# Second half of the mixing projection row tile by row tile, with part of its weights loaded during the merge and later element-wise work moved to VectorE

## The chip, the core and the metric

The kernel runs on one core of a Trainium2 chip. The metric is the time of one execution in microseconds (us), measured on the device. TensorE is called PE, VectorE DVE, ScalarE ACT, GpSimd POOL and SyncE SP, as in the profile. SP, POOL and ACT also issue DMAs from queues that each work in their own order.

## The reference

One layer of a streaming encoder on x of 1024 x 1024 in float32, with weights of the layer and a conditioning vector that gives shifts, scales and gates.

```python
h = _layer_norm(x) * (1.0 + sc1) + sh1
q_a, k_a, v_a, f_a, q_c, k_c, v_c, gate_a, gate_c = jnp.split(h @ w_in[l], split_points, axis=-1)
o_a = _forgetting_attention(...)
o_c = _chunk_band_attention(...)
merged = (jax.nn.sigmoid(gate_a) * (o_a @ w_br_fox[l]) + jax.nn.sigmoid(gate_c) * (o_c @ w_br_chunk[l]))
mix = merged @ w_out[l]
x = _layer_norm(alpha * x + (1.0 + g1) * mix, ln1_g[l], ln1_b[l])
h = _layer_norm(x) * (1.0 + sc2) + sh2
u = _causal_depthwise_conv(h @ w_up[l], conv_w[l], conv_b[l])
a, val = jnp.split(u, 2, axis=-1)
y = (jax.nn.silu(a) * val) @ w_down[l]
x = _layer_norm(alpha * x + (1.0 + g2) * y, ln2_g[l], ln2_b[l])
```

The lines that matter here are the merge, the mix, the first LayerNorm, and the start of the FFN (`h @ w_up`).

## The kernel before, in words

Every float32 operand of a product is parted into a high part (a cast) and a low part (the operand less its high part), and every product is made of three matmuls, high by high, high by low and low by high, on 128 x 512 tiles. So a step needs a cast (mostly on ACT) and a subtraction (on DVE or POOL) before PE can start. Weights that the kernel has already parted in DRAM are read back as two 512 KB tiles, `wh` and `wl`, by `parted_w`; of each three such pairs, one lies in tiles called `ws`.

The 1024 rows are handled in two halves of 512. `merge(half)` makes eight products (c = 0 to 7) of the two branch outputs with the branch weights `brd[c]`, each from one weight pair and one gate tile `sgl`; DVE multiplies by the gate (`sgl`), adds, and parts the result into `mh` and `ml`. `mix(half)` multiplies the eight merged tiles by the eight steps of `w_out` (`wod[k]`, k = 0 to 7) into eight PSUM tiles: four row tiles of 128 rows, two halves of 512 columns each, called `psm`. Then, for each row tile, DVE makes the residual sum into `xr`, whose rows of x were loaded by SP.

In the first half all steps run over all four row tiles. In the second half (mix 1), steps 0 to 3 run over all row tiles, and steps 4 to 7 tile by tile, with weights in a pool `wide` that is opened only once the attention outputs' pool is closed, at the end of merge 1. Beside mix 1, `turned_0` transposes the first half's normalised rows on PE into the FFN operands `ha`, `hb`. `norms(half)` applies the first LayerNorm with its gain and bias (`l1g`, `l1b`), stores the rows to `xd`, and normalises them once more into x tiles. For the first half this lies beside merge 1; for the second half it lies after mix 1, beside the first four `head` calls. A `head(c)` is one of eight early products of the FFN, 24 matmuls into `psu`, which use only the first half's operands; `ready(c)` loads and parts its weights. `EARLY = 4` heads run before the second half's operands exist.

After that `turned_1` transposes the second half's rows and forms, for each of four column tiles j, five parted operands: the tile itself (h_22) and four sums or differences (h_t1 to h_t4), with `put` doing the difference (`ht`), the cast and the low part (`hc`). The remaining four heads are interleaved with it. Then the pools `th` and `mxb`, which hold those sums, are closed, and the memory becomes weight tiles `wx` of the FFN loop, whose products (L851) fill the rest of the program. All instructions are placed on their engines in one order by a scheduler at build time; an engine never overtakes itself, nor does a DMA queue.

Of the kernel before, what the change touches and what calls it, by code (L numbers as in the profile page):

```python
# [19 lines left out]
P = 128  # L20
# [15 lines left out]
EARLY = 4  # L36
# [8 lines left out]
def body(ctx, tc, a, out):  # L45
# [814 lines left out]
    def ready(c):  # L860
        if c < HEAD:
            w11, w12 = raw(c, 0, wp, "ws")
            raws.clear()
            lo = ve if c >= EARLY else po
            readied.append((operand(head_slot, mxb, w11, lo=lo), operand(head_slot, mxb, w12, lo=lo)))

    def head(c):
        w11, w12 = readied.pop(0)
        p1 = None
        for i in range(2):  # L870
            ps = product((w11, w12)[i], (h_11, h_21)[i])
            if c < EARLY:
                t = mxb.tile([P, H], F32, name=nm("mc"), tag="h32", bufs=4)
            else:
                t = yp.tile([P, H], F32, name=nm("mc"), tag="mc", bufs=3)
            if i == 0:
                se.copy(out=t, in_=ps)
                p1 = t
            else:
                ve.tensor_tensor(out=t, in0=ps, in1=p1, op=ALU.add)  # L880
            se.dma_start(out=md[c, i], in_=t)
        ready(c + 2)

    if True:
# [11 lines left out]
        def merge(half, os_, beside):  # L896
# [15 lines left out]
            for c in range(KD):  # L912
# [9 lines left out]
                for _ in range(3):  # L922
                    next(beside, None)
            return ms

        def mix(half, ms, beside, wide=None, ended=None):
# [5 lines left out]
            def add(t, k, w):  # L932
                mh, ml = ms[k]
                ts = slice(t * P, (t + 1) * P)
                for n in range(2):
                    pe.matmul(ps[t][n], mh[:, ts], w[0][:, n, :], start=k == 0, stop=False)
                    pe.matmul(ps[t][n], mh[:, ts], w[1][:, n, :], start=False, stop=False)
                    pe.matmul(ps[t][n], ml[:, ts], w[0][:, n, :], start=False, stop=k == KD - 1)

            late = []  # L940
            for k in range(KD):
                last = wide and k >= KD - 4
                w = parted_w(wod[k], wide if last else None)
                if last:
                    late.append((k, w))
                    continue
                for t in range(4):
                    add(t, k, w)
                next(beside, None)
            xs = []  # L950
            for t in range(4):
# [3 lines left out]
                xs.append(xx)  # L955
            for t in range(4):
# [11 lines left out]
        def norms(half, xs, xn):  # L968
            for t, xx in enumerate(xs):
                if half:  # L970
                    normalise(xx, xx, True)
                    ve.tensor_tensor(out=xx, in0=xx, in1=l1g, op=ALU.mult)
                    yield
                    po.tensor_tensor(out=xx, in0=xx, in1=l1b, op=ALU.add)
                else:
                    mv, r = norm_scale(xx)
                    ve.scalar_tensor_tensor(out=xx, in0=xx, scalar=mv[:, 0:1], in1=l1g, op0=ALU.subtract, op1=ALU.mult)
                    ve.scalar_tensor_tensor(out=xx, in0=xx, scalar=r, in1=l1b, op0=ALU.mult, op1=ALU.add)
                    yield
# [34 lines left out]
        def turned_1(tiles):  # L1014
            for j in range(4):
# [5 lines left out]
                t1 = put(h_t1[j], x, h11, ALU.subtract, (ve, se, po), th, 6)  # L1021
                t2 = put(h_t2[j], y, t1, ALU.subtract, (ve, se, po), th, 6)
                put(h_t3[j], y, x, ALU.subtract, (po, se, ve), th, 6)
# [10 lines left out]
        x0, x1 = [], []  # L1034
        beside = norms(0, xs0, x0)
        m1 = merge(1, o1, beside)
# [3 lines left out]
        wide_cm, wide = opened(name="wide", bufs=4, side="right")  # L1040
# [4 lines left out]
        ready(0)  # L1045
        ready(1)
# [5 lines left out]

    mx_cm.__exit__(None, None, None)
    wide_cm.__exit__(None, None, None)
# [377 lines left out]
```

## Time and profile before

| | value |
|---|---|
| median of three runs | 1600.44 us |
| the runs | 1605.11, 1599.81, 1600.44 us |
| profiled execution | 1605.72 us, span 1603.9 us |
| PE busy in the span | 1521.6 us (95%), 7663 instructions |
| DVE busy | 1080.8 us (67%) |
| ACT busy | 712.5 us (44%) |
| POOL busy | 687.1 us (43%) |
| mean granted PE clock | 0.979 of full speed |
| moved by DMA | 317.81 MB, mean 198 GB/s |

The span is the stretch of the profile from the first to the last instruction; the profiled execution's time is 1.8 us longer. Times of stretches below are us from the start of the span. Busy shares are means over stages with different limits, so they say little on a single stage.

### The profile page before, as it was taken

The page shows a single profiled execution, that of the slowest core. Times are in us where ns is not written, and L with a number is a line of the kernel's source. Part 1 is how long each engine was busy: PE and PEld are TensorE (multiplying, and loading weights), DVE is VectorE, ACT ScalarE, POOL GpSimd, SP SyncE. Part 2 cuts the span into 40 slices and gives each one's busy share as a digit, 9 for nine tenths or more (in the row PEclk, how much of TensorE's full clock was granted, in tenths as well). Part 3 has the DMA queues.
Part 4 walks back from the last instruction along what each step waited for, and adds up shares of the span by engine and source line. Part 5 has one row for each costly group of instructions (what it writes and reads, how often), then busy time and mean ns, then how long its engine had stood idle before and what let it go on. Part 6 is the DMA issues. An engine that isn't in the chain of part 4 may idle for free.

```text
span 1603.9 us, 21885 instructions
## 1 busy us (share of the span) xinstructions
PE 1521.6 (95%) x7663; PEld 1276.3 (80%) x7663; DVE 1080.8 (67%) x2138; ACT 712.5 (44%) x1322; POOL 687.1 (43%) x606
## 2 busy tenths in 40 slices
PE   6899999999999899899999986999999999999996
PEld 3788888789888888788878864888888888788885
DVE  6748566567767666564548498577777876746698
ACT  3446444454444444352102156354445544555451
POOL 1139898888676876200000135644554554000000
PEclk9999999999999999999999998999999999999998
DMA  9036665756666678526999755334442233697552
GB/s 369 32 126 219 228 202 204 232 194 198 210 208 202 230 271 270 181 93 230 309 322 318 272 202 185 119 127 168 159 138 105 99 120 113 213 346 259 192 188 74
DMA packets 130398, 317.81 MB, mean 198 GB/s; under 512 B 12896, under 2 KB 21808, under 8 KB 130288
## 3 DMA queue, kind: packets, MB, share of 16 engines
q1 hardware_dynamic: 94480, 208.84, 38.5%
q0 software_dynamic: 24144, 87.83, 16.0%
q10 hardware_dynamic: 11664, 19.75, 3.3%
q8 instruction: 60, 0.98, 0.3%
q14 instruction: 50, 0.41, 0.1%
HBM read 223.73 MB, written 84.25 MB: 192 GB/s over the span
## 4 chain that ended last, share of the span: by engine, by line
PE 76%; DVE 12%; DMA 6%; ACT 2%; issue 2%; POOL 1%; SPq 0%; DVEq 0%; ACTq 0%; POOLq 0%
PE psu L851 23%; PE psd L1249 4%; PE psd L1250 4%; PE psd L1248 4%; PE pso L502 4%; PE pst L488 3%; PE psg L192 3%; PE psg L193 3%; PE psg L194 3%; PE psq L192 2%; PE psq L193 2%; PE psq L194 2%; DMA cb<-in_rel_t 2%; PE psv L294 2%; PE psv L295 2%
## 5 line engine op out<-in xcount | busy, mean ns | idle before, releaser
L851 PE MATMUL psu<-hc,wx 128*128 128x512 f32 x720 | 171.1, 393 | 11.4 <-ACT wx L839 9.5
L851 PEld LDWEIGHTS psu<-hc,wx 128*128 128x128 f32 x720 | 136.5, 190 | 40.9 <-ACT wx L839 9.9
L1097 DVE SCALAR_TENSOR_TENSOR pcv<-u,convp,pcv 128x1024 f32<-128x1024 f32 x88 | 113.1, 1286 | 45.6 <-ACT pcv L1095 44.7
L454 ACT ACTIVATE s<-s,mx 128x640 f32<-128x640 f32 (+7 forms) x128 | 94.5, 738 | 83.5 <-DVE mx L448 81.7
L1238 DVE TENSOR_TENSOR op<-rw,op 128x512 fp32r<-128x512 f32 x146 | 93.4, 686 | 52.8 <-ACT op L1237 52.4
L1237 ACT CAST op<-rw 128x512 fp32r<-128x512 f32 x146 | 85.2, 622 | 83.8 <-PE psd L1250 41.8
L1249 PE MATMUL psd<-op,op 128*128 128x512 f32 x292 | 113.7, 389 | 1.0 <-DVE op L1238 1.0
L1248 PE MATMUL psd<-op,op 128*128 128x512 f32 x292 | 113.6, 389 | 0.0
L1250 PE MATMUL psd<-op,op 128*128 128x512 f32 x292 | 113.6, 389 | 0.0
L491 ACT CAST pt<-pst 128x512 fp32r<-128x512 f32 (+1 forms) x192 | 82.5, 450 | 67.0 <-PE pst L488 65.5
L192 PE MATMUL psg<-h1h,wh 128*128 128x512 f32 x256 | 105.7, 413 | 0.0
L192 PE MATMUL psq<-h1h,wh 128*128 128x512 f32 x256 | 105.1, 412 | 0.4 <-DVE h1h L188 0.4
L492 DVE TENSOR_TENSOR pt<-pst,pt 128x512 fp32r<-128x512 f32 (+1 forms) x192 | 96.4, 518 | 12.6 <-ACT pt L491 10.7
L193 PE MATMUL psq<-h1l,wh 128*128 128x512 f32 x256 | 101.8, 398 | 1.8 <-DVE h1l L189 1.8
L193 PE MATMUL psg<-h1l,wh 128*128 128x512 f32 x256 | 101.8, 398 | 0.0
L194 PE MATMUL psg<-h1h,wl 128*128 128x512 f32 x256 | 101.6, 397 | 0.0
L194 PE MATMUL psq<-h1h,wl 128*128 128x512 f32 x256 | 101.2, 395 | 0.3 <-DVE wl L112 0.3
L502 PE MATMUL pso<-pt,vs 128*128 128x256 f32 x608 | 93.5, 292 | 7.9 <-DVE pt L492 7.8
L502 PEld LDWEIGHTS pso<-pt,vs 128*128 128x128 f32 x608 | 82.9, 194 | 17.1 <-DVE pt L492 10.7
L550 POOL TENSOR_SCALAR dr<-dr,cond 128x512 f32<-128x512 f32 x56 | 91.6, 1637 | 11.3 <-DMA dr<-in_w_ada 10.4
L488 PE MATMUL pst<-ident,s 128*128 128x128 f32 x528 | 84.1, 276 | 12.2 <-DVE pt L492 12.1
L980 POOL DMA_DIRECT2D xd<-xr x8 | 4.5, 559 | 205.6 <-DVE t L129 192.2
(284 smaller groups left out, 4107.4 us busy)
## 6 DMA issues: line engine op xcount, KB each, us to landing
ws<-in_w_up SPq DMA_DIRECT2D x36, 512.0 KB, 3.8
dr<-in_w_ada POOLq DMA_DIRECT2D x32, 512.0 KB, 4.3
dr<-in_w_down POOLq DMA_DIRECT2D x22, 512.0 KB, 5.5
td<-dr POOLq DMA_DIRECT2D x22, 512.0 KB, 5.5
rw<-td SPq DMA_DIRECT2D x44, 256.0 KB, 4.5
yd<-y SPq DMA_DIRECT2D x20, 512.0 KB, 3.2
rw<-yd SPq DMA_DIRECT2D x40, 256.0 KB, 3.9
rw<-sd SPq DMA_DIRECT2D x33, 256.0 KB, 4.6
```

The source lines that it names most:

```text
L192: pe.matmul(ps, wh, xh, start=start, stop=False)
L193: pe.matmul(ps, wh, xl, start=False, stop=False)
L194: pe.matmul(ps, wl, xh, start=False, stop=stop)
L454: se.activation(out=st[:, 0:nk], in_=st[:, 0:nk], func=AF.Exp, scale=-1.0, bias=prev, accum_out=sums[:, col : col + 1])
L488: pe.transpose(ps[:, b * P : (b + 1) * P], st[:, c0 : c0 + P], ident)
L492: ve.tensor_sub(out=dl, in0=src, in1=dh)
L502: pe.matmul(ps[:, 0:256], vs[:, h % 2, j0 + j, :], pt[j // 4][:, c, j % 4, :], start=j == 0 and c == 0, stop=j == nj - 1 and c == 1)
L851: pe.matmul(ps, w[:, a_, k, :], h[k][b_], start=first, stop=k == 3 and a_ == 1, skip_group_check=on)
L1097: ve.scalar_tensor_tensor(out=ps, in0=u[b][:, 2 - d : S + 2 - d], scalar=cp[:, 2 - d : 3 - d], in1=ps, op0=ALU.mult, op1=ALU.add)
L1248: pe.matmul(ps[t], g[:, 0, ts], d[:, 0], start=start, stop=False, skip_group_check=on)
L1249: pe.matmul(ps[t], g[:, 0, ts], d[:, 1], start=False, stop=False, skip_group_check=on)
L1250: pe.matmul(ps[t], g[:, 1, ts], d[:, 0], start=False, stop=stop, skip_group_check=on)
```

## The change: what it does

1. **Mix 1 by row tiles.** Step 0 runs over all four row tiles; then for each row tile the steps 1, 2, 4, 5, 6, 7, 3. Seven of eight steps are now tile by tile, where four were.
2. **Weights of steps 4 to 7 loaded ahead.** The pool `wide` is opened before merge 1, and a generator `widened`, advanced once for each product of merge 1, issues eight loads of 512 KB on SP's queue from the third product on. The rows of x and step 3's weights are loaded after steps 1 and 2.
3. **Second normalisation on VectorE.** For the second half, `norms` used ACT to normalise, DVE to multiply by the gain and POOL to add the bias; now it uses two wide DVE instructions with two inputs each, as the first half already did.
4. **Operand sums on VectorE.** In `turned_1` three instructions for each j, which are twelve in all, move from POOL to DVE: the low parts of t1 and t2 and the difference of t3.
5. **First heads' weights in mix 1.** Three heads' weights are loaded on POOL's queue into a pool `hd`, cast on ACT and parted on DVE, one 128 x 1024 instruction each, during mix 1. `EARLY` is 3, and the weights of heads 3 and 4 are made ready after mix 1. All low parts of head weights are now on DVE.

The core of the diff:

```diff
-EARLY = 4
+EARLY = 3
@@ ready
-            lo = ve if c >= EARLY else po
-            readied.append((operand(head_slot, mxb, w11, lo=lo), operand(head_slot, mxb, w12, lo=lo)))
+            readied.append((operand(head_slot, mxb, w11, lo=ve), operand(head_slot, mxb, w12, lo=ve)))
+            return
+        st = pool.tile([P, KD, P], F32, name=nm("hs"), tag="hs", bufs=2)
+        po.dma_start(out=st, in_=a["w_up"][2 * c])
+        w = pool.tile([P, 2, KD, P], F32R, name=nm("hw"), tag="hw", bufs=EARLY)
+        se.copy(out=w[:, 0], in_=st)
+        ve.tensor_sub(out=w[:, 1], in0=st, in1=w[:, 0])
+        readied.append((w[:, :, 0:4], w[:, :, 4:8]))
@@ head
-        ready(c + 2)
+        if c >= EARLY:
+            ready(c + 2)
@@ mix
+            end = 3 if wide else KD - 1
             late = []
-            for k in range(KD):
-                last = wide and k >= KD - 4
-                w = parted_w(wod[k], wide if last else None)
-                if last:
-                    late.append((k, w))
-                    continue
+            for k in range(1 if wide else KD):
+                w = parted_w(wod[k])
                 for t in range(4):
                     add(t, k, w)
                 next(beside, None)
+            if wide:
+                late += [(k, parted_w(wod[k])) for k in (1, 2)] + sorted(wide.items())
...
+            if wide:
+                late.append((3, parted_w(wod[3])))
@@ norms
-                if half:
-                    normalise(xx, xx, True)
-                    ve.tensor_tensor(out=xx, in0=xx, in1=l1g, op=ALU.mult)
-                    yield
-                    po.tensor_tensor(out=xx, in0=xx, in1=l1b, op=ALU.add)
-                else:
-                    mv, r = norm_scale(xx)
...
+                mv, r = norm_scale(xx)
+                ve.scalar_tensor_tensor(out=xx, in0=xx, scalar=mv[:, 0:1], in1=l1g, op0=ALU.subtract, op1=ALU.mult)
+                ve.scalar_tensor_tensor(out=xx, in0=xx, scalar=r, in1=l1b, op0=ALU.mult, op1=ALU.add)
+                yield
@@ turned_1
-                t1 = put(h_t1[j], x, h11, ALU.subtract, (ve, se, po), th, 6)
-                t2 = put(h_t2[j], y, t1, ALU.subtract, (ve, se, po), th, 6)
-                put(h_t3[j], y, x, ALU.subtract, (po, se, ve), th, 6)
+                t1 = put(h_t1[j], x, h11, ALU.subtract, (ve, se, ve), th, 6)
+                t2 = put(h_t2[j], y, t1, ALU.subtract, (ve, se, ve), th, 6)
+                put(h_t3[j], y, x, ALU.subtract, (ve, se, ve), th, 6)
@@ main program
+        wide_cm, widep = opened(name="wide", bufs=4)
+        wide = {}
+        def widened():
+            yield
+            yield
+            for k in range(4, KD):
+                wide[k] = parted_w(wod[k], widep)
+                yield
-        m1 = merge(1, o1, beside)
+        m1 = merge(1, o1, beside, widened())
...
-        wide_cm, wide = opened(name="wide", bufs=4, side="right")
+        hd_cm, hdp = opened(name="hd", bufs=1, side="right")
+        for c in range(EARLY):
+            ready(c, hdp)
...
-        ready(0)
-        ready(1)
+        ready(EARLY)
+        ready(EARLY + 1)
```

Line numbers shift by up to 19 lines after the change; in the rows below L903 is `parted_w`'s load, L913 the gate tile's, L1005 and L1008 are `put`'s difference and low part, L870 is the new load of head weights and L986 the store to `xd`.

**SP's queue in merge 1.** The names are tiles and where they are loaded from: `brd` are branch weights, `gd` gates, `wod` weights of the mix. Before:

```order
L893 DMA wh_8885<-brd 128x2x512
L893 DMA wl_8886<-brd 128x2x512
L893 DMA wh_8964<-brd 128x2x512
L893 DMA wl_8965<-brd 128x2x512
L903 DMA sgl_8883<-gd 128x2x512
L893 DMA ws_9003<-brd 128x2x512
L893 DMA ws_9004<-brd 128x2x512
L893 DMA wh_9042<-brd 128x2x512
L893 DMA wl_9043<-brd 128x2x512
L903 DMA sgl_8962<-gd 128x2x512
```

and after the change:

```order
L903 DMA wh_8888<-brd 128x2x512
L903 DMA wl_8889<-brd 128x2x512
L903 DMA wh_8965<-wod 128x2x512
L903 DMA wl_8966<-wod 128x2x512
L913 DMA sgl_8886<-gd 128x2x512
L903 DMA wh_8971<-brd 128x2x512
L903 DMA wl_8972<-brd 128x2x512
L903 DMA wh_9008<-wod 128x2x512
L903 DMA wl_9009<-wod 128x2x512
L903 DMA ws_9014<-brd 128x2x512
L903 DMA ws_9015<-brd 128x2x512
L913 DMA sgl_8969<-gd 128x2x512
```

Between the same two gate tiles there were two pairs of branch weights, and now there are two pairs of branch weights and a pair of mix weights, with another ahead of the first gate tile in place of a branch pair.

**DVE at the start of `turned_1`.** `ht` are the sums and differences of j = 0, `hc` low parts, `h` the transposed tile, `hf` a first-half tile read back, and `wh`, `wl` low parts of a head's weights. Before:

```order
L999 TENSOR_TENSOR ht_9912<-h_2016_9901,hf_9892 128x512
L999 TENSOR_TENSOR ht_9916<-h_2018_9908,ht_9912 128x512
L1002 TENSOR_TENSOR hc_9850<-h_2018_9908,hc_9849 128x512
L999 TENSOR_TENSOR ht_9924<-hf_9893,ht_9916 128x512
L1002 TENSOR_TENSOR hc_9874<-ht_9920,hc_9873 128x512
L1002 TENSOR_TENSOR hc_9882<-ht_9924,hc_9881 128x512
L840 TENSOR_TENSOR wl_9969<-ws_9964,wl_9969 128x512
```

and after the change:

```order
L1005 TENSOR_TENSOR ht_9855<-h_2002_9844,hf_9835 128x512
L1008 TENSOR_TENSOR hc_9793<-h_2004_9851,hc_9792 128x512
L1005 TENSOR_TENSOR ht_9859<-h_2004_9851,ht_9855 128x512
L1005 TENSOR_TENSOR ht_9863<-h_2004_9851,h_2002_9844 128x512
L1008 TENSOR_TENSOR hc_9801<-ht_9855,hc_9800 128x512
L1008 TENSOR_TENSOR hc_9809<-ht_9859,hc_9808 128x512
L1008 TENSOR_TENSOR hc_9817<-ht_9863,hc_9816 128x512
L1005 TENSOR_TENSOR ht_9867<-hf_9836,ht_9859 128x512
L840 TENSOR_TENSOR wh_9909<-ws_9907,wh_9909 128x512
L840 TENSOR_TENSOR wl_9912<-ws_9907,wl_9912 128x512
L1008 TENSOR_TENSOR hc_9825<-ht_9867,hc_9824 128x512
```

What stood on POOL now stands between the other instructions of DVE, and the low parts of a head's weights come within the chain. From the first of these rows to the last low part of j = 3 there are now 46 instructions on DVE.

**POOL from mix 1 to the first FFN products.** Before, the last rows of it up to the second column tile (`xd` is the store of normalised rows):

```order
L980 DMA xd<-xr_9303 128x1024
L999 TENSOR_TENSOR ht_9920<-h_2018_9908,h_2016_9901 128x512
L1002 TENSOR_TENSOR hc_9858<-ht_9912,hc_9857 128x512
L1002 TENSOR_TENSOR hc_9866<-ht_9916,hc_9865 128x512
L999 TENSOR_TENSOR ht_10000<-h_2037_9988,h_2035_9981 128x512
```

and after the change, from merge 1's end up to the first FFN weight:

```order
L870 DMA hs_9180<-in_w_up 128x1024
L870 DMA hs_9185<-in_w_up 128x1024
L870 DMA hs_9190<-in_w_up 128x1024
L986 DMA xd<-xr_9239 128x1024
L986 DMA xd<-xr_9241 128x1024
L986 DMA xd<-xr_9243 128x1024
L986 DMA xd<-xr_9245 128x1024
L840 TENSOR_TENSOR wl_10196<-ws_9871,wl_10196 128x512
```

POOL now issues three loads and four stores there, and its next computing instruction belongs to the FFN.

## Rows read from the trace of the kernel before

**Rows 1.** Windows, stretches (us): merge 1, mix 1, normalisation to first FFN products, the rest.

```profile
core 0: us, PE busy (x) PEld busy (x) DVE busy (x) ACT busy (x) POOL busy (x), PEclk, DMA share, GB/s
832.00:880.00 48.00, 46.22 (x196) 37.49 (x195) 43.29 (x109) 9.91 (x17) 2.19 (x4) 0.96 0.90 320
880.00:929.00 49.00, 47.22 (x210) 38.67 (x210) 24.18 (x50) 12.29 (x20) 8.01 (x6) 0.97 0.71 258
929.00:1010.00 81.00, 60.86 (x266) 47.16 (x264) 66.20 (x106) 46.18 (x78) 43.08 (x34) 0.89 0.55 194
1010.00:1590.00 580.00, 579.04 (x2554) 479.07 (x2555) 423.15 (x552) 283.75 (x430) 180.64 (x136) 1.00 0.46 162
```

**Rows 2.** Waits of PE in 929 to 1010: line, releaser, us in total, times, longest.

```profile
PE psu L851 <- ACT wx L839: 9.5, 1, 9.5
PE pst L990 <- ACT x L140: 2.9, 1, 2.9
PE psu L851 <- ACT wh L839: 2.3, 1, 2.3
PE psu L851 <- POOL wx L840: 1.9, 1, 1.9
```

**Rows 3.** Timeline of PE, 989 to 1012: start, us, instructions; in brackets idle before, releaser.

```profile
989.08 0.84 PE L851 MATMUL psu<-hb,wl 128*128 128x512 f32 x3
999.39 1.22 PE L851 MATMUL psu<-hc,wx 128*128 128x512 f32 x2 [9.47 <-ACT wx L839]
1002.49 7.12 PE L851 MATMUL psu<-hc,wx 128*128 128x512 f32 x22 [1.88 <-POOL wx L840]
```

**Rows 4.** Windows, the pst transposes alone, at the end of mix 1.

```profile
928.80:930.50 1.70, 1.64 (x16) 1.64 (x15) 0.00 (x0) 1.01 (x2) 1.00 0.00 0
```

**Rows 5.** Timeline of DVE at the start of `turned_1`, same columns as rows 3.

```profile
967.57 0.68 DVE L840 TENSOR_TENSOR wh<-ws,wh 128x512 fp32r<-128x512 f32 x1
968.17 1.77 DVE L999 TENSOR_TENSOR ht<-h,hf 128x512 f32<-128x512 f32 x1
970.05 0.69 DVE L999 TENSOR_TENSOR ht<-h,ht 128x512 f32<-128x512 f32 x1
```

**Rows 6.** Timeline of POOL over the same stretch.

```profile
968.09 1.31 POOL L999 TENSOR_TENSOR ht<-h,h 128x512 f32<-128x512 f32 x1 [11.31 <-ACT h L992]
970.68 3.52 POOL L1002 TENSOR_TENSOR hc<-ht,hc 128x512 fp32r<-128x512 f32 x2 [1.29 <-ACT hc L1001]
```

**Rows 7.** Timeline of DVE, inside `turned_1` and at its end.

```profile
983.21 0.68 DVE L840 TENSOR_TENSOR wh<-ws,wh 128x512 fp32r<-128x512 f32 x1
983.81 0.68 DVE L840 TENSOR_TENSOR wl<-ws,wl 128x512 fp32r<-128x512 f32 x1
...
997.57 1.45 DVE L1002 TENSOR_TENSOR hc<-ht,hc 128x512 fp32r<-128x512 f32 x2
```

**Rows 8.** Windows of four short stretches, columns as in rows 1.

```profile
826.00:834.00 8.00, 6.50 (x29) 5.06 (x27) 6.22 (x11) 0.00 (x0) 0.00 (x0) 1.00 1.03 393
838.00:850.00 12.00, 12.00 (x52) 9.84 (x51) 11.06 (x28) 1.25 (x4) 0.57 (x1) 0.95 0.70 240
850.00:874.00 24.00, 24.00 (x108) 19.87 (x107) 23.07 (x68) 8.03 (x13) 1.62 (x3) 1.00 1.00 357
883.60:886.90 3.30, 3.30 (x10) 2.53 (x9) 1.45 (x3) 0.62 (x1) 0.00 (x0) 0.50 0.99 361
```

**Rows 9.** DMA issues in 836 to 880: KB each, median us to landing.

```profile
xr<-in_x SPq DMA_DIRECT2D x2, 512.0 KB, 7.6
```

**Rows 10.** Waits of SP, which issues DMAs, in 832 to 886.

```profile
SPq L893 <- PE psb L194: 23.1, 7, 7.8
SPq L903 <- DVE ml L920: 6.5, 3, 3.5
```

**Rows 11.** Timeline of PE, the first wait in mix 1.

```profile
883.12 0.50 PE L936 MATMUL psm<-wh,mh 128*128 128x512 f32 x1 [1.78 <-DVE sgl L910]
```

**Rows 12.** Timeline of DVE, one wide normalisation step in merge 1.

```profile
857.45 1.26 DVE L977 SCALAR_TENSOR_TENSOR xr<-xr,mv,l1g 128x1024 f32<-128x1024 f32 x1
```

More of the change, by code (lines that the diff above doesn't have):

```diff
@@ L858, in body, with ready @@
     readied = []
-    def ready(c):
-        if c < HEAD:
+    def ready(c, pool=None):
+        if c >= HEAD:
+            return
+        if pool is None:
             w11, w12 = raw(c, 0, wp, "ws")
             raws.clear()
-            lo = ve if c >= EARLY else po
-            readied.append((operand(head_slot, mxb, w11, lo=lo), operand(head_slot, mxb, w12, lo=lo)))
+            readied.append((operand(head_slot, mxb, w11, lo=ve), operand(head_slot, mxb, w12, lo=ve)))
+            return
+        st = pool.tile([P, KD, P], F32, name=nm("hs"), tag="hs", bufs=2)
[4 more added lines that the diff above has]
+        readied.append((w[:, :, 0:4], w[:, :, 4:8]))
     def head(c):
@@ L894, in parted_w, with merge @@
             return parts
-        def merge(half, os_, beside):
+        def merge(half, os_, beside, ahead=iter(())):
             ms = []
@@ L923, in merge @@
                     next(beside, None)
+                next(ahead, None)
             return ms
@@ L937, in add @@
                     pe.matmul(ps[t][n], mh[:, ts], w[1][:, n, :], start=False, stop=False)
-                    pe.matmul(ps[t][n], ml[:, ts], w[0][:, n, :], start=False, stop=k == KD - 1)
+                    pe.matmul(ps[t][n], ml[:, ts], w[0][:, n, :], start=False, stop=k == end)
+            end = 3 if wide else KD - 1
             late = []
-            for k in range(KD):
-                last = wide and k >= KD - 4
-                w = parted_w(wod[k], wide if last else None)
-                if last:
-                    late.append((k, w))
-                    continue
+            for k in range(1 if wide else KD):
+                w = parted_w(wod[k])
                 for t in range(4):
@@ L969, in norms @@
             for t, xx in enumerate(xs):
-                if half:
-                    normalise(xx, xx, True)
-                    ve.tensor_tensor(out=xx, in0=xx, in1=l1g, op=ALU.mult)
-                    yield
-                    po.tensor_tensor(out=xx, in0=xx, in1=l1b, op=ALU.add)
-                else:
-                    mv, r = norm_scale(xx)
-                    ve.scalar_tensor_tensor(out=xx, in0=xx, scalar=mv[:, 0:1], in1=l1g, op0=ALU.subtract, op1=ALU.mult)
-                    ve.scalar_tensor_tensor(out=xx, in0=xx, scalar=r, in1=l1b, op0=ALU.mult, op1=ALU.add)
-                    yield
+                mv, r = norm_scale(xx)
+                ve.scalar_tensor_tensor(out=xx, in0=xx, scalar=mv[:, 0:1], in1=l1g, op0=ALU.subtract, op1=ALU.mult)
+                ve.scalar_tensor_tensor(out=xx, in0=xx, scalar=r, in1=l1b, op0=ALU.mult, op1=ALU.add)
+                yield
                 po.dma_start(out=xd[4 * half + t], in_=xx)
@@ L1051, in body @@
             pass
+    wide_cm.__exit__(None, None, None)
     mx_cm.__exit__(None, None, None)
-    wide_cm.__exit__(None, None, None)
+    hd_cm.__exit__(None, None, None)
     yp_cm, yp = opened(name="yp", bufs=3, side="right")
```

## The prediction

> **What bounds the kernel now.** I read the windows first. From 1010 us to 1590 PE is busy 579 of 580 us at the full granted clock [rows 1], in an order that hardly changes, so what starts the FFN loop earlier carries one to one to the end. Merge 1 and mix 1 (832 to 929) are nearly full too. The loose stretch is 929 to 1010, with PE busy 60.9 of 81 us at a mean granted clock of 0.89. The waits there show 9.5 us for the first FFN weight operand `wx`, 2.9 us for the normalised rows x and 2.3 for a head weight [rows 2]; the timeline of PE puts the longest at 990 to 999 and the end of the first 24 FFN matmuls at 1002.49 + 7.12 = 1009.6 [rows 3].
>
> Call T the end of mix 1, 929.0 before. From T to those 24 matmuls' end were 80.6 us. The work in it is eight heads and the two FFN products, 216 matmuls, at 579.0 / 2554 = 0.227 us each [rows 1], which is 49 us, and 48 transposes, of which 16 took some 2 us with their surroundings [rows 4], which is 6 us. So 55 us were needed and about 25 lost, of which the four longest waits are 16.6 [rows 2].
>
> Why is `wx` late? Its memory belongs to the pools of `turned_1`, and comes free when DVE ends the sums. DVE ran that part from 968.17 [rows 5] to 997.57 + 1.45 = 999.0 [rows 7], 30.8 us without a pause. A 128x512 subtraction with two inputs in SBUF took 0.69 us, and starts followed each other at 0.60 (983.21, 983.81) [rows 7], but the one that began at 968.17 took 1.77 us [rows 5], while POOL ran an instruction of the same kind from 968.09 on for 1.31 [rows 6]. So POOL's help stretched the chain that it was meant to shorten.
>
> **Part 4, the operand sums.** POOL loses 12 instructions and DVE gains them; together with the heads' low parts the row of DVE from the first sum to the last low part holds 46. At 0.60 us a start [rows 7] they take 27.6 us against 30.8. That holds if the long ones came from POOL. The old chain had 30 instructions in DVE's row, 18 us at 0.60, so 12.8 us were lost in it; if that came of ACT's hand-offs and stays whole, the new chain takes 27.6 + 12.8 = 40.4. I take 0.60, since the pairs at 0.60 [rows 7] are the same operation, between POOL's instructions. The Trainium skill, "SBUF — State Buffer", section "Who interferes with whom", says that a VectorE instruction with two SBUF inputs contends with a GpSimd instruction that reads SBUF, and that the later one blocks until the first ends. The 1.77 against 0.69 agrees in kind, and by that rule the chain would be the 27.6.
>
> **Parts 3 and 5, T to the chain.** After T, PE has 16 transposes (2.1 us with gaps, [rows 4]) and three heads, 72 x 0.227 = 16.3, whose weights are there; with half a us of waiting for the first operands' low parts they end at T + 18.9. Before, `ready(0)` and `ready(1)` began only after the mix, and one of their products waited 2.3 [rows 2]. Of the first three x tiles the first normalisation is now within the mix, whose tiles end 42 x 0.227 = 9.5 us apart. DVE's row from the last residual to the last x tile's scale holds 23 instructions of 0.60, two of 1.26 [rows 12] and some thirty tiny ones at about 0.1: 19 us, and ACT's last tile makes T + 22. Its transposes stand behind 18 of head 3's 24 matmuls, at T + 18.9 + 4.1 + 0.8 = T + 23.8, so the 2.9 for x goes. Head 3 and the transposes end at T + 25.4, its sum on DVE at T + 26.6, where the chain begins: before at T + 39.2. The chain ends at T + 54.2.
>
> PE meanwhile needs heads 4 to 7, 21.7, and 24 transposes, 3, from T + 25.4, with some 2 us of waiting for low parts that queue in DVE's chain: T + 52. The first FFN operand is now in a `wl` slot, which isn't in the released memory, and needs only t2, four rows before the chain's end; the second is a `wx`, cast (0.6) and parted on POOL (1.3, as POOL's instruction in [rows 6]) after T + 54.2. So the first 24 matmuls take from about T + 53 to T + 60.5, with a us of waiting in it. The floor is the 55 us of bare work; the ceiling, with the 40.4 us chain, T + 73.3. The step is worth 60.5 - 80.6 = **-20.1 us** (-25.6 to -7.3).
>
> Casts on ACT and low parts on DVE of three heads in mix 1 are three of about 1.25 us each on engines busy 12 and 24 of 49 us [rows 1]. They delay the first residual to some 4 us later, while the next use of its PSUM lies some 9 us on; with that cover gone they would cost 4. Their three loads, on POOL's queue ahead of the stores to `xd`, take 3 x 1.33 us of DMA in a stage at a share of 0.71 [rows 1], which moreover loses eight weight loads: nothing, or at most those 4 us if they came late.
>
> **Parts 1 and 2, merge 1 and the mix.** The eight added loads are 4.19 MB: at the 393 GB/s of the first stretch in [rows 8], 10.7 us of all DMA engines. From 832 to 880 those were busy 0.90 at 320 GB/s [rows 1], 15.4 MB, and full from 850 on; the room of 4.8 us lies mostly in 838 to 850 at 0.70 [rows 8]. Two loads of x rows [rows 9] leave that stretch, 2.7 us. So on throughput 15.4 + 4.2 - 1.05 = 18.5 MB at 393 need 47.2 us, 0.8 less than the stretch: bound below, no loss but a start at -0.8. At the 357 of 850 to 874 [rows 8] they need 51.9, +3.9. The queue is worse than throughput, for SP issues in order and waited 23.1 us for weight tiles and 6.5 for gate tiles [rows 10]. Walking SP's order at 1.33 us a transfer, with each gate tile held until DVE frees it, product 5's weights come 4 us late, product 6's another 1.3, product 7's 0.9: about +5.9 at the merge's end, where adding all 10.7 is the upper bound. I take 5.9. Each gap also brings a slower clock: after the wait of 1.78 us [rows 11], PE ran from 883.6 to 886.9 at a granted clock of 0.50 [rows 8], the lower of its two levels, which loses 1.65 us. One such wait is added (+1.7); the one of 1.78 with its 1.65 goes, since merge 1's last tile `ml` isn't needed so soon and its gate is done: -3.5. So mix 1 ends **4.1 us later** (-4 to +11), at 933.1. Its own 192 matmuls stay. Step 3's weights, now last of SP's queue, land about as they are needed, 1 us at most.
>
> The Trainium skill, "DMA: Bandwidth & Descriptors", section "Where 436 GB/s comes from", puts the limit between HBM and one core at about 358 GB/s. The trace has 357 in one stretch [rows 8] and 393 in another, so by that rule the +3.9 would be a floor of the merge's loss and the net 1 to 2 us less favourable; the 393 speaks against it as a hard limit.
>
> **Sum.** 4.1 - 20.1 = -16.0. On the profiled execution's 1605.72 (span 1603.9 and 1.8 around it) that is 1589.7. That execution is 5.3 us above the median of the runs, 1600.44, so the forecast for a median is 1600.44 - 16.0 = **1584.5**.
>
> **The rivals.** (B) *Merge 1 starved for the whole of the added loads*: +10.5 in place of 4.1, net -9.6, 1590.8. For it speaks the DMA share of 1.00 from 850 to 874; against it the room before 850. (C) *The sums are no faster on DVE*, since ACT's casts between them or the waits on transposes set the pace: with some 10 of the 12.8 us still lost, T + 70.5, net -6.0, 1594.4; with all of them -3.2. For it: DVE was already the busiest there (66.2 of 81 us [rows 1]). Against: the pairs at 0.60. The skill's rule on the shared port, named above, speaks against this rival too. (D) *Each merge product waits*: the mix's weights stand in SP's queue ahead of the branch weights that PE wants next, so that each of six products (c = 2 to 7) waits for its weights and PE then runs 3.3 us at the lower clock after each gap. It decides when the merge's cost is over 20.1 + 3.5 = 23.6 us, 3.9 for each product, thus gaps of 2.3 us; at 3.5 us of gap it is 6 x 5.15 = 31, net +7.4 and **1608**, slower; at 3 us +4.6, about the same. Against it: the transfers added are only 10.7 us, so the queue's blocking would have to double them. (E) *Nothing queues*: merge -0.8 with the 3.5 gone as well, and PE near its floor: -21 to -26, about 1577.
>
> **How the numbers follow.** What a measurement of this kernel can tell from no change is some 0.3%, 4.8 us. Chances: forecast 0.55 (1579 to 1589), B 0.13, C 0.14, D 0.10, E 0.08. All of the forecast, B and E and most of C (0.09) are faster by more than that, D gives 0.08 slower, and the rest of C and D 0.07 the same. The range of 1576 to 1598 holds the forecast, B, C and the near half of E, and leaves out D and the far end of E.
>
> **What the profile after would show.** If right: the first 24 FFN matmuls end about 60 us after mix 1's end; POOL has no L1008; DVE's `turned_1` subtractions are 0.68 to 0.69 us each and the chain is under 29 us; no wait of PE for `wx` over 2 us; waits of 3 to 5 us for `wh`, `wl` from `brd` about product 5 of merge 1, and mix 1's end near 933. Wrong: subtractions at 1.2 to 1.8 with POOL idle (C); many waits of 3 us on `brd` with the clock at 0.50 behind each (D); waits for head weights `wh` in DVE's chain that keep PE at a low clock beside it; or a last x tile later than T + 24.

## The result and the profile after

The changed kernel takes 1587.70 us, the median of nine runs (1583.16 to 1590.82), against 1600.44 for nine runs of the kernel before (1592.34 to 1610.54). The ratio is 0.9915, with a 95% interval of 0.9895 to 0.9935, so it is 13.6 us faster (10.4 to 16.8). The forecast was 1584.5.

The profiled spans differ by more, 1603.9 against 1581.4. So I compare stages, each by PE's own instructions: merge 1 from its first to the end of its last `psb` matmul, mix 1 from there to the end of the last `psm` matmul, then to the end of the 216th `psu` matmul (eight heads and the two FFN products), then the rest of the span. Before, merge 1 began at 834.18, and in the changed kernel at 823.83; those 10.4 us lie in code that is not changed, and the kernels below begin it anywhere from 823.8 to 846.7. That the three stages come to 13.6 as well as the medians is partly chance, for merge 1 and mix 1 repeat only within some 3 us from profile to profile (see the run with part 4 alone).

| us | merge 1 | mix 1 | to the 24 FFN products | rest | sum of the first three |
|---|---|---|---|---|---|
| before | 45.80 | 49.04 | 80.59 | 594.3 | 175.4 |
| after | 54.40 | 48.24 | 59.19 | 595.7 | 161.8 |
| difference | +8.6 | -0.8 | -21.4 | +1.4 | -13.6 |

The windows of the changed kernel over the same four stretches answer to [rows 1]:

```profile
core 0: us, PE busy (x) PEld busy (x) DVE busy (x) ACT busy (x) POOL busy (x), PEclk, DMA share, GB/s
823.80:878.20 54.40, 47.15 (x193) 36.88 (x194) 45.27 (x112) 11.14 (x19) 3.25 (x6) 0.97 0.93 340
878.20:926.50 48.30, 46.50 (x211) 37.43 (x210) 31.41 (x55) 11.14 (x18) 2.14 (x4) 1.00 0.54 210
926.50:985.70 59.20, 55.73 (x265) 45.02 (x264) 52.02 (x110) 40.48 (x69) 9.11 (x10) 1.00 0.69 228
985.70:1570.00 584.30, 580.44 (x2556) 479.14 (x2554) 427.32 (x562) 285.67 (x433) 184.21 (x139) 1.00 0.47 163
```

PE is busy 55.7 of 59.2 us in the third stretch, where it was busy 60.9 of 81, and the granted clock is 1.00 where the mean was 0.89. The waits of PE from mix 1's end to 1010 answer to [rows 2]:

```profile
PE psu L851 <- ACT wx L839: 1.7, 1, 1.7
PE psu L851 <- DVE wh L840: 1.2, 1, 1.2
PE psu L851 <- POOL wx L840: 0.6, 1, 0.6
```

The 9.5 us for `wx` have become 1.7, and the wait for x is gone. In the timeline of PE (answering to [rows 3]) the first FFN product, on a `wl` slot, begins right behind the heads and the second waits for its `wx`:

```profile
972.46 2.60 PE L851 MATMUL psu<-ha,wh 128*128 128x512 f32 x10 [1.19 <-DVE wh L840]
...
977.17 2.88 PE L851 MATMUL psu<-hc,wl 128*128 128x512 f32 x12
981.70 0.73 PE L851 MATMUL psu<-hc,wx 128*128 128x512 f32 x2 [1.65 <-ACT wx L839]
983.06 1.21 PE L851 MATMUL psu<-hc,wx 128*128 128x512 f32 x4 [0.63 <-POOL wx L840]
```

The timeline of DVE shows why, and answers to [rows 5] and [rows 7]:

```profile
951.86 0.68 DVE L1005 TENSOR_TENSOR ht<-h,hf 128x512 f32<-128x512 f32 x1
952.46 0.69 DVE L1008 TENSOR_TENSOR hc<-h,hc 128x512 fp32r<-128x512 f32 x1
953.06 0.69 DVE L1005 TENSOR_TENSOR ht<-h,ht 128x512 f32<-128x512 f32 x1
...
956.67 0.69 DVE L840 TENSOR_TENSOR wh<-ws,wh 128x512 fp32r<-128x512 f32 x1
...
974.71 1.21 DVE L1005 TENSOR_TENSOR ht<-h,ht 128x512 f32<-128x512 f32 x1
975.84 1.78 DVE L1008 TENSOR_TENSOR hc<-ht,hc 128x512 fp32r<-128x512 f32 x1
...
980.55 0.68 DVE L1008 TENSOR_TENSOR hc<-ht,hc 128x512 fp32r<-128x512 f32 x1
```

The subtractions take 0.68 to 0.70 us but for two, starts follow at 0.60, and the chain runs from 951.86 to 980.55 + 0.68 = 981.23: 29.4 us for 46 instructions, where 27.6 was forecast. The two at 974.71 and 975.84, 1.21 and 1.78 us long, make 1.6 of the 1.8 us over the forecast. They run beside POOL's first two subtractions for FFN weights, whose timeline is:

```profile
972.73 2.64 POOL L840 TENSOR_TENSOR wl<-ws,wl 128x512 fp32r<-128x512 f32 x1 [32.12 <-ACT wl L839]
975.34 1.73 POOL L840 TENSOR_TENSOR wh<-ws,wh 128x512 fp32r<-128x512 f32 x1
```

Merge 1 is where the kernel lost. PE's longest waits from its start to 890:

```profile
PE psb L192 <- DVE y L127: 2.9, 1, 2.9
...
PE psb L192 <- DMA ws<-brd: 1.6, 1, 1.6
...
PE psm L948 <- DMA wl<-wod: 1.0, 2, 0.7
```

The first, put down to DVE, is a DMA: DVE's small instruction had little to do with `psb`, and the branch weights `wh` of that product landed only at 858.71, 0.13 us ahead of the matmul at 858.84. From 858 to 862, behind that gap, the mean granted clock was 0.63. Landing had become slow, as the DMA issues in 842 to 860 show (KB each, median us to landing):

```profile
wh<-brd SPq DMA_DIRECT2D x2, 512.0 KB, 9.9
wl<-brd SPq DMA_DIRECT2D x2, 512.0 KB, 10.6
```

SP meanwhile stood 35.5 us before gate tiles that DVE still held (823 to 890), where it had been 6.5 in [rows 10]. The DMA share in that part of the merge was 0.74 and then full:

```profile
834.00:844.00 10.00, 9.07 (x41) 7.17 (x40) 9.99 (x25) 1.22 (x4) 1.11 (x2) 1.00 0.74 250
844.00:858.00 14.00, 9.45 (x40) 6.89 (x38) 14.00 (x43) 4.06 (x7) 1.07 (x2) 1.00 1.04 406
```

### The profile page after: what moved, and what is told of

It is laid out like the page before. It is cut to its first block, busy times and chain, and to the rows that moved or that the text cites. A ratio compares the mean times of both kernels' runs of the same rounds, so it can differ in the third digit from the quotient of the medians.

```text
span 1581.4 us, 21839 instructions
## 1 busy us (share of the span) xinstructions
PE 1513.7 (96%) x7663; PEld 1268.8 (80%) x7663; DVE 1076.0 (68%) x2155; ACT 707.8 (45%) x1315; POOL 653.6 (41%) x585
## 4 chain that ended last, share of the span: by engine, by line
PE 77%; DVE 12%; DMA 5%; issue 2%; ACT 2%; SPq 0%; POOL 0%; DVEq 0%; POOLq 0%; ACTq 0%
PE psu L851 23%; PE psd L1268 4%; PE psd L1269 4%; PE psd L1267 4%; PE pso L502 4%; PE psg L192 3%; PE psg L193 3%; PE psg L194 3%; PE pst L488 3%; PE psq L193 2%; PE psq L192 2%; PE psq L194 2%; PE psv L294 2%; PE psv L295 2%; PE psv L296 2%
## 5 line engine op out<-in xcount | busy, mean ns | idle before, releaser
L851 PE MATMUL psu<-hc,wx 128*128 128x512 f32 x696 | 163.7, 389 | 2.3 <-ACT wx L839 1.7
L851 PEld LDWEIGHTS psu<-hc,wx 128*128 128x128 f32 x696 | 130.5, 188 | 30.1 <-ACT wx L839 2.1
L986 POOL DMA_DIRECT2D xd<-xr x8 | 4.3, 542 | 253.5 <-DVE t L129 188.7
L492 DVE TENSOR_TENSOR pt<-pst,pt 128x512 fp32r<-128x512 f32 (+1 forms) x192 | 96.5, 519 | 11.8 <-ACT pt L491 10.1
```

Source lines behind the costliest of these rows:

```text
L492: ve.tensor_sub(out=dl, in0=src, in1=dh)
L851: pe.matmul(ps, w[:, a_, k, :], h[k][b_], start=first, stop=k == 3 and a_ == 1, skip_group_check=on)
```

## Experiments

Five of the runs undo one part of the change each, or were meant to; "stage" is the third column above. Each ratio is to runs of the kernel before made together with that run. The intervals are 3 to 7 us to either side, so most differences between these kernels are read from stages, of one profile each. The stage repeats well: it took 59.1 or 59.2 us in the changed kernel and in five kernels below that edit only loads, stores and buffers (60.4 and 62.1 in two more).

**Part 4 undone: the sums on POOL again.**

```diff
-t1 = put(h_t1[j], x, h11, ALU.subtract, (ve, se, ve), th, 6)
+t1 = put(h_t1[j], x, h11, ALU.subtract, (ve, se, po), th, 6)
...
-put(h_t3[j], y, x, ALU.subtract, (ve, se, ve), th, 6)
+put(h_t3[j], y, x, ALU.subtract, (po, se, ve), th, 6)
```

> The changed kernel with part 4 undone: the low parts of t1 and t2 and the difference of t3 are on POOL again, all else as changed. Theory (POOL's instructions stretch DVE's): subtractions of DVE beside a POOL instruction take 1.2 to 1.8 us again instead of 0.69, so the chain, though 12 instructions shorter, takes 31 us or more against 26.7, and from mix 1's end to the end of the first 24 FFN products it takes 64 to 70 us against 59; the kernel is 5 to 11 us slower than the changed one, so 2 to 8 us faster than the one before. Rival (the gain of that stage is only the earlier start of the chain and the fewer waits of heads): less than 2 us slower than the changed one.

Median 1593.2, ratio to the kernel before 0.9944 (0.9906 to 0.9982). The stage took 66.4 us, +7.2, and the three stages 168.3, +6.5 on the changed kernel. Its timelines of DVE and then of POOL, in the second column tile:

```profile
959.06 0.68 DVE L840 TENSOR_TENSOR wh<-ws,wh 128x512 fp32r<-128x512 f32 x1
959.66 0.68 DVE L840 TENSOR_TENSOR wl<-ws,wl 128x512 fp32r<-128x512 f32 x1
960.26 1.78 DVE L1005 TENSOR_TENSOR ht<-h,hf 128x512 f32<-128x512 f32 x1
962.14 0.69 DVE L1005 TENSOR_TENSOR ht<-h,ht 128x512 f32<-128x512 f32 x1
```

```profile
960.02 1.47 POOL L1005 TENSOR_TENSOR ht<-h,h 128x512 f32<-128x512 f32 x1 [2.03 <-ACT h L998]
```

Two subtractions at 0.60 while POOL is idle, then one of 1.78 us while POOL runs one of 1.47 that began 0.24 us earlier, then 0.69 again. DVE's chain had 33 instructions in 31.8 us, against 46 in 29.4. The theory of the stretched instructions holds. The Trainium skill, "SBUF — State Buffer", section "Who interferes with whom", says so for a VectorE instruction with two SBUF inputs beside a GpSimd instruction that reads SBUF; the later one waits until the other ends. By that rule DVE's would have taken, as an estimate, 1.47 - 0.24 + 0.69 = 1.92 us; it took 1.78.

**Part 4 alone, on the kernel before** (the same three lines, the other way).

> The kernel before with part 4 alone: the low parts of t1 and t2 and the difference of t3 on DVE in place of POOL, nothing else. Theory (POOL's instructions stretch DVE's): the chain falls from 30.8 us to 42 instructions at 0.60, 25 us, its start stays at 39 us behind mix 1's end, so the stage from there to the end of the first 24 FFN products falls from 80.6 to 74 to 76 us, the kernel by 5 to 7. Rival (the sums were not the bound, the chain's start was): the stage stays within 2 us of 80.6.

Median 1595.65, ratio 0.9974 (0.9954 to 0.9994). The stage fell from 80.6 to 75.9, and the chain from 30.8 to 25.0 us, as expected; it still began 39.2 us behind the mix. PE's waits behind mix 1:

```profile
PE psu L851 <- ACT wx L839: 6.1, 1, 6.1
PE psu L851 <- POOL wx L840: 3.9, 1, 3.9
```

The first wait for `wx` is 6.1 where it was 9.5, the second, for POOL's low part, 3.9 where it was 1.9. So the faster chain is worth 4.7 us by itself, and 7.2 where the earlier start has put PE close behind it.

Merge and mix took 45.03 and 46.95 us, 2.9 less than in the profile before, though nothing in them is edited; that is the size of what single profiles leave open there. The wait of [rows 11], 1.78 us with a granted clock of 0.50 behind it, has no equal in this run: PE's waits for `sgl` in its mix are two that come to 1.0, and the clock is 1.00 over merge and mix, where it was 0.96 and 0.97.

```profile
PE psm L936 <- DVE sgl L910: 1.0, 2, 0.6
```

**Part 3 undone: the second normalisation on ACT, DVE and POOL.**

```diff
+if half:
+    normalise(xx, xx, True)
+    ve.tensor_tensor(out=xx, in0=xx, in1=l1g, op=ALU.mult)
+    yield
+    po.tensor_tensor(out=xx, in0=xx, in1=l1b, op=ALU.add)
...
```

> The changed kernel with part 3 undone: the second half's rows are normalised on ACT, multiplied on DVE and added to on POOL again. Theory (the last x tile had two us to spare): that tile comes 2 to 4 us later, PE waits 0 to 3 us for it, the kernel is 0 to 3 us slower than the changed one. Rival (the wide steps on DVE were worth much, since POOL's wide additions stretch DVE's instructions in mix 1 and behind it): 5 us or more slower.

Median 1594.15, ratio 0.9921 (0.9883 to 0.996). The last x tile ended 25.9 us behind the mix instead of 22.0, and PE waited for it; the stage grew by 2.7 us. The three stages grew by 1.3, since merge and mix were 1.4 shorter, which is within what single profiles leave open. PE's waits there:

```profile
PE psu L851 <- DVE ha L1014: 1.5, 1, 1.5
...
PE pst L1002 <- ACT x L140: 0.8, 1, 0.8
```

**Part 5 undone: the heads' weights behind the mix** (three early heads kept).

```diff
-for c in range(EARLY):
-    ready(c, hdp)
...
-ready(EARLY)
-ready(EARLY + 1)
+ready(0)
+ready(1)
...
```

> The changed kernel with part 5 undone but for the count of early heads (three): their weights are loaded on SP's queue and parted after mix 1, in the weight pool's slots, with the low parts on DVE. Theory: the first head waits 1 to 3 us for its operands and each of the next two 1 to 2 us, DVE has six more low parts ahead of the x tiles (3.6 us), so the stage from mix 1's end to the first 24 FFN products grows by 3 to 8 us, as does the time. Rival (those weights were ready anyway, the waits of before came from POOL's slow low parts): within 2 us of the changed one.

Median 1593.55, ratio 0.9946 (0.9912 to 0.9981). The stage grew by 10.1 us, more than expected, and the three stages by 8.0. The first heads did not wait: they ended 18.2 us behind the mix in both kernels. But DVE's low parts stood between the rows of the last x tile, which ended at 28.3 us instead of 22.0; the chain began at 32.2 instead of 25.4 and ended at 59.9 instead of 54.8. That is 5.1 of the 10.1 us. The other 5.0 lie between the chain's end and the stage's: the first FFN product, which was on a `wl` slot and did not wait, is on `wx` here, as in the kernel before, and waits. So the edit undid two things. PE's waits and that product's row in its timeline:

```profile
PE psu L851 <- ACT wx L839: 2.7, 1, 2.7
PE psu L851 <- POOL wx L840: 2.0, 1, 2.0
PE psu L851 <- ACT wh L839: 1.9, 1, 1.9
```

```profile
984.71 1.01 PE L851 MATMUL psu<-hc,wx 128*128 128x512 f32 x3 [2.67 <-ACT wx L839]
```

**Part 1 undone: steps 0 to 3 over all row tiles.**

```diff
-for k in range(1 if wide else KD):
+for k in range(4 if wide else KD):
...
-late += [(k, parted_w(wod[k])) for k in (1, 2)] + sorted(wide.items())
+late += sorted(wide.items())
...
```

> The changed kernel with part 1 undone: steps 0 to 3 over all row tiles and 4 to 7 tile by tile, as before, with the latter's weights still loaded ahead. Theory: row tiles end 5.5 us apart instead of 9.5, DVE needs about 7 us for residual and norm of each, so some 5 us of it move behind the mix, the last x tile comes late and the stage from mix 1's end to the first 24 FFN products grows from 59 to 61 to 65 us; the mix itself stays within 2 us. Rival (the tile order was worth nothing, early norms were hidden in either order): that stage stays within 1 us of 59.

Median 1590.58, ratio 0.9918 (0.989 to 0.9946). The stage grew by 2.9 to 62.1, with the last x tile at 25.1 instead of 22.0 as the theory had it, but the mix was 1.6 shorter: the three stages took 162.7, +0.9. So tile order is worth 2.9 us in the stage; whether the mix really pays 1.6 of it back is within what single profiles leave open.

**Part 2 undone in half: the weights of steps 4 to 7 written behind merge 1.**

```diff
-m1 = merge(1, o1, beside, widened())
+m1 = merge(1, o1, beside)
...
-late += [(k, parted_w(wod[k])) for k in (1, 2)] + sorted(wide.items())
+late += [(k, parted_w(wod[k])) for k in (1, 2)] + [(k, parted_w(wod[k], wide)) for k in range(4, KD)]
...
```

> The changed kernel with part 2 undone: the weights of steps 4 to 7 are loaded behind merge 1, right after steps 1 and 2, into the same pool. Theory: merge 1 falls back from 55.5 to about 47.5 us, and mix 1 grows from 48.2 to 57 to 62, since its first row tile wants fourteen tiles of weights at once and the eight moved ones take 10.7 us at 1.33 each; net 1 to 6 us slower than the changed kernel. Rival (the loads are hidden there as well, so that loading ahead only cost): 4 to 8 us faster than the changed one.

The edit did less than it says. The pool `wide` is open during merge 1, and the scheduler still placed the four loads of steps 4 and 5 in merge 1 (823.95 to 868.90), at 836.74, 842.00, 847.30 and the second of the two at 857.86; the order of loads in the program that this kernel builds names them. Only steps 6 and 7 were loaded behind it, from 872.05 to 874.65. The timeline of SP:

```profile
836.74 0.45 SPq L903 DMA_DIRECT2D wh<-wod  x1
842.00 0.54 SPq L903 DMA_DIRECT2D wl<-wod  x1
847.30 0.56 SPq L903 DMA_DIRECT2D wh<-wod  x1
...
857.86 0.94 SPq L903 DMA_DIRECT2D wl<-wod  x2
...
872.05 1.52 SPq L903 DMA_DIRECT2D wh<-wod  x1
```

Median 1587.67, ratio 0.9913 (0.9881 to 0.9945). Merge 1 fell by 9.5 us, the mix grew by 4.2 and the stage by 2.9: 159.5 in all, 2.4 less than the changed kernel, with the same median. The 2.4 lie within what single profiles leave open. So four of the eight loads fitted into the merge without a wait of PE's there, and with all eight it took 9.5 us longer; the expected net of +1 to +6 did not come, and what the kernel takes with none of the loads ahead was not run. Windows of its merge 1 and mix 1, and PE's wait in the mix:

```profile
823.95:868.90 44.95, 44.72 (x193) 36.05 (x194) 40.18 (x105) 9.90 (x17) 3.25 (x6) 1.00 0.97 357
868.90:921.30 52.40, 47.50 (x210) 38.87 (x210) 31.36 (x57) 12.09 (x20) 1.06 (x2) 0.93 0.61 225
```

```profile
PE psm L947 <- DVE sgl L920: 4.9, 1, 4.9
```

PE is busy 44.7 of 44.95 us in the merge. The mix lost less than thought, and its 4.9 us wait is for the last gate sums, not for the weights.

**Three buffers for the gate tile**, to see whether the queue or the bytes make the merge slow.

```diff
-sg = mx.tile([P, 2, H], F32, name=nm("sgl"), tag="sgl", bufs=2)
+sg = mx.tile([P, 2, H], F32, name=nm("sgl"), tag="sgl", bufs=3)
```

> The changed kernel with three buffers for the gate tile in place of two. Theory of the queue (SP stood 35 us before gate tiles whose buffer DVE still held, and the weights behind them were issued late): merge 1 falls from 54.4 to 50 to 52 us. Rival, throughput (the DMA engines are full in merge 1 by the added loads alone): merge 1 stays at 54 us, within 1 us.

Median 1585.4, ratio 0.9909 (0.9885 to 0.9934); merge 1 48.3, the three stages 155.2, 6.7 less than the changed kernel. That would speak for the queue, but the edit did more than it says. The timeline of SP shows a load of the mix's weights before merge 0 began (749.0 in this kernel), the first of four, for steps 4 and 5:

```profile
737.90 0.45 SPq L903 DMA_DIRECT2D wh<-wod  x1
```

So half of the added bytes had left merge 1, and this run does not tell queue from bytes.

**The first half's stores behind the merge**, with two gate buffers and with three.

```diff
-po.dma_start(out=xd[4 * half + t], in_=xx)
+if half:
+    po.dma_start(out=xd[4 * half + t], in_=xx)
...
+for t in range(4):
+    po.dma_start(out=xd[t], in_=xs0[t])
```

> The changed kernel with the four stores of the first half's rows, 512 KB each, issued behind merge 1 instead of within it. Theory of throughput: 5.3 us of DMA less in merge 1, which falls from 54.4 to 49 to 51 us; mix 1 grows by 0 to 3, since its x rows wait for the stores. Rival, the queue (SP blocked by gate tiles): merge 1 falls by less than 2 us.

> Three gate buffers and the four stores of the first half's rows behind merge 1. With two buffers the late stores did nothing (merge 1 at 53.8). Theory: with the queue mended the DMA engines bind, so 5.3 us of transfers less bring merge 1 from 48.3 to 45 to 47 us. Rival (what is left is order or DVE): merge 1 within 0.7 us of 48.3.

Ratios 0.9948 (0.9922 to 0.9974) and 0.9883 (0.9842 to 0.9924), medians 1589.64 and 1581.37. Neither tells what it was to tell: the scheduler put the stores where they had been, 14.2 us into the merge in the first (840.71 against a start of 826.47; 14.0 in the changed kernel). The timeline of POOL:

```profile
840.71 0.57 POOL L1058 DMA_DIRECT2D xd<-xr  x1 [193.03 <-DVE t L129]
```

They stand as repeats of the kernels without that edit: merge 1 took 53.8 and 54.4 us in the one pair, 49.8 and 48.3 in the other. In the first pair the three stages are 162.0 and 161.8 us, and yet the ratios, 0.9948 and 0.9915, lie 5 us apart: so much the timed runs leave open between two kernels.

**The eight loads on ACT's queue**, with two gate buffers and with three.

```diff
-sy.dma_start(out=x.bitcast(F32), in_=src[j : j + 2].rearrange("j p n -> p j n"))
+(se if pool else sy).dma_start(out=x.bitcast(F32), in_=src[j : j + 2].rearrange("j p n -> p j n"))
```

> The changed kernel with the eight loads of steps 4 to 7 on ACT's queue in place of SP's; two gate buffers. SP's order in merge 1 is then word for word that of the kernel before, and the bytes are those of the changed one. Theory of the queue (the added loads pushed a pair of branch weights behind each gate tile): merge 1 falls from 54.4 to 46 to 50 us. Rival, the bytes: merge 1 stays within 1.5 us of 54.

> The changed kernel with both: the eight loads on ACT's queue and three gate buffers. If SP's order was the whole cost, merge 1 is at 45.5 to 47 us and the kernel 7 to 10 us faster than the changed one; if the bytes bind once the order is mended, merge 1 stays at 48 and the kernel 5 to 7 faster.

Medians 1600.01 and 1593.06, ratios 0.9975 (0.9949 to 1.0) and 0.9941 (0.9922 to 0.9961). Merge 1 took 45.6 and 45.9 us, but this is not the queue's doing: ACT's queue was free early, and all eight loads were issued in merge 0, the first here (timeline of ACT):

```profile
756.29 0.38 ACTq L903 DMA_DIRECT2D wh<-wod  x1
```

Merge 0 and mix 0 then took 97.0 us and 98.5, where they took 88.3 in the changed kernel. Windows of that stretch with the loads on ACT's queue, then of the changed kernel, and PE's longest wait in the first:

```profile
749.70:846.70 97.00, 89.80 (x385) 73.12 (x384) 37.26 (x50) 11.05 (x14) 0.00 (x0) 0.96 1.00 336
```

```profile
735.50:823.80 88.30, 87.24 (x385) 71.92 (x384) 37.16 (x50) 11.05 (x14) 0.00 (x0) 1.00 0.95 320
```

```profile
PE psb L192 <- DMA wh<-brd: 4.5, 1, 4.5
```

The loss of 8.6 us was moved, not mended: the DMA share is 0.95 there even without the added loads.

**Loads written behind the merge and three gate buffers.**

```diff
-tag="sgl", bufs=2)
+tag="sgl", bufs=3)
...
-late += [(k, parted_w(wod[k])) for k in (1, 2)] + sorted(wide.items())
+late += [(k, parted_w(wod[k])) for k in (1, 2)] + [(k, parted_w(wod[k], wide)) for k in range(4, KD)]
...
```

> Loads of steps 4 to 7 behind the merge, and three buffers for the gate tile. Without the third buffer the mix began with 4.9 us of waiting for the last gate sums, whose tiles were issued late, and a half clock behind it. Theory: that wait shrinks to under 2 us, the mix falls from 52.4 to 47 to 50 us, merge 1 stays at 45, and the kernel is 2 to 5 us faster than without the buffer, so 4 to 8 us faster than the changed one. Rival (the weights of the mix come late anyway, so PE waits for those instead): the sum of merge and mix stays within 1 us of 97.4.

Median 1584.87, ratio 0.9914 (0.988 to 0.9947). The wait for gate sums fell from 4.9 to 0.2 us, but the mix stayed at 50.9 with waits for its weights, and merge and mix took 96.95 against 97.36. That is the rival's number, but not its case: in this kernel no load of steps 4 to 7 lay behind the merge. Those of steps 4 and 5 were issued from 728.03 on, before merge 0, and those of steps 6 and 7 in merge 1 (828.5 to 874.5), the last of them at 871.8. So its loads lie much as in the run with three gate buffers alone. The stage fell from 62.1 to 59.1, so the three stages took 156.1, 3.4 less than without the buffer and 5.8 less than the changed kernel.

**Bytes and merge 1.** Rate times length of the window gives what was moved in merge 1. The changed kernel moved 340 x 54.4 = 18.5 MB and the kernel with half of the loads behind the merge 357 x 44.95 = 16.0 (windows above). Three gate buffers with the loads written behind the merge, with them ahead, and with them ahead and the stores' edit:

```profile
828.50:874.50 46.00, 45.69 (x193) 37.22 (x194) 42.74 (x109) 10.74 (x18) 3.26 (x6) 0.96 0.93 341
```

```profile
838.20:886.50 48.30, 46.41 (x193) 37.05 (x194) 43.97 (x111) 11.36 (x19) 3.26 (x6) 0.96 0.94 345
```

```profile
826.90:876.60 49.70, 46.77 (x193) 36.97 (x194) 45.02 (x113) 11.36 (x19) 3.26 (x6) 0.97 0.94 342
```

These are 15.7, 16.7 and 17.0 MB in 46.0, 48.3 and 49.7 us. At the 357 GB/s of the merge that PE filled, 16.0 MB take 44.9 us, and 16.7, 17.0 and 18.5 take 46.7, 47.6 and 51.9; measured were 1.6, 2.1 and 2.5 us more. So bytes could explain most of the merge's length, and order, buffers and the lower clock behind a gap the last two us. This is argued from windows and not shown: no run changed bytes or order alone, a merge that is long for another reason has time to move more, and in a merge that PE filled, 357 is what was asked for, which need not be the most that could be had. The Trainium skill, "DMA: Bandwidth & Descriptors", section "Where 436 GB/s comes from", gives about 358 GB/s for one core's share of HBM, which is near the rate of the filled merge; but 844 to 858 in the changed kernel moved 406 for 14 us, so it is no hard limit of a stretch.

## Why the prediction was right, and where it was off

**What bounds the kernel: right.** The stage behind mix 1 gave the gain, and it carried to the end but for 1.4 us, which were not foreseen. The trace shows 0.9 of them: behind the stage PE waited 0.7 and 0.4 us for the FFN's `u` tiles, where it had waited 0.2.

**Parts 3 to 5, T to the 24 products: right in place and size.** Forecast -20.1, measured -21.4, and each step can be set beside its forecast, behind the mix's end: three heads at 18.2 (18.9), the last x tile at 22.0 (22), head 3 at 24.7 (25.4), the chain from 25.4 to 54.8 (26.6 to 54.2), the 24 products at 59.2 (60.5). The 60.5 is a slip, for the forecast's own terms, 53 + 24 x 0.227 + 1, give 59.5. The chain was to stay under 29 us and took 29.4: POOL's first work for the FFN begins inside the chain and stretches two of DVE's instructions, which the forecast did not price. Rival C is refuted by the runs with the sums on POOL and with the sums alone. That parts 5 and 4 carry most of the gain (10.1 and 7.2 us of the stage when undone) and parts 3 and 1 less (2.7 and 2.9) is shown as well. That early weights matter through DVE's row ahead of the last x tile, and not by the heads' waits, was only half in the forecast, which counted those 19 us without saying that six low parts more would lengthen them; and 5.0 of the 10.1 go with the first product's `wl` slot.

**Parts 1 and 2: the right sign, mis-sized.** The term "4.1 us later" measured 7.8 against the profile before (+8.6 in the merge, -0.8 in the mix). Against merge and mix of the run with part 4 alone, where their code is the same, it is 10.7 (+9.4 and +1.3).

The merge itself was nearly right: 5.9 by the queue and 1.7 for one gap with its slow clock are 7.6, where 8.6 or 9.4 were measured. The byte count is right partly by chance. The forecast's 18.5 MB were counted for the 48 us from 832 to 880; merge 1 proper moved 14.5 MB before and 18.5 after, and 1.05 MB of that are two of the heads' loads of part 5, issued at 875.17 and 875.75, which the forecast had in the mix.

The step that failed most is the 3.5 us taken off in the mix for the wait at [rows 11] and the clock behind it. It was read from one execution, and in the run with part 4 alone the same code has no such wait. In the changed kernel the wait for `sgl` is gone, but PE waits 1.8 us for the mix's own weights instead, 1.0 for `wl` in the row above and 0.8 for `ws`, and the mix gave back 0.8 and not 3.5.

Rival B's 10.5 is 2.7 too high by the one profile and fits by the other, so its size is not refuted. Rival D did not come: there were waits for branch weights, but far from six of 3 us. That the median came within 3.2 us of the forecast is partly luck, as the loss of parts 1 and 2 was put too low and the gain of parts 3 to 5 too low as well.

The stage's losses when one part is undone (10.1, 7.2, 2.9 and 2.7 us for parts 5, 4, 1 and 3) come to more than the 21.4 gained; they overlap and can't be added. For part 2 no worth is shown: the kernel with half of it undone has the same median, 1587.67, and stages 2.4 us shorter, which is within what single profiles leave open.

**A faster version.** Three gate buffers on the changed kernel give stages 5.4 to 6.7 us shorter (161.8 to 156.4 and 155.2, in two kernels of that form) and ratios to the kernel before of 0.9909 and 0.9883. Those intervals overlap with that of the changed kernel, so by the timed runs it is not settled that it beats it. By the stages it does, most of it in a merge with fewer bytes; but four of the loads were then moved before merge 0, and what they cost there lies outside these stages and was not measured.

What stays open: how much of the merge's loss is SP's order, since each edit that was to part it from the bytes was placed elsewhere by the scheduler; and what the kernel takes with none of the eight loads in merge 1 or before it.

## What to carry to other kernels

Where an engine helps another by taking element-wise work off it, look at the lengths of the helped engine's instructions while the helper runs: here 12 instructions more on DVE made its chain shorter. Before loads are put ahead of their use, add their bytes to what that stretch moves already and divide by the rate of a stretch that was full, not by the best rate; here PE had no wait within the merge with half of the added loads, and lost 9.5 us there with all of them. Before a wait is counted as a gain, see whether another profile of the same code has it. And after an edit of buffers or queues, read where the scheduler has put the transfers before taking the time for the theory's.

## What was unexpected of the hardware

A full DMA stretch had no one rate: 357 GB/s over the 45 us of a merge that PE filled, 406 over 14 us of the changed one, 336 at a share of 1.00 over merge 0 and mix 0 with eight loads more. Loads and stores were mixed differently in each, and no run parts the two. And the same eight loads cost about the same in either place: 8.6 us in merge 1, and 8.7 and 10.2 in merge 0 and mix 0, though they were on another queue there.
